# A two-layer streaming encoder step: mask rows sent between the latent queries, three norm biases added on VectorE, weight sums two products later

## The chip, the core and the metric

The kernel runs on one core of a Trainium2 chip. The metric is the device time of one launch in microseconds (us), the median of three runs, lower is better. TensorE (PE, with its weight loads as PEld), VectorE (DVE), ScalarE (ACT) and GpSimd (POOL) work through their own instruction streams in order; SyncE (SP) issues the DMAs in its own order.

## The reference, cut to what matters

1024 prompt frames and 64 sample frames (1088 rows, `T`) go through two layers with `D` = 1024. Layer 0 mixes by two head groups, of which A is latent attention with a rotary part and a chunk mask; layer 1 mixes by stick-breaking attention. After each mixer and each MLP stands a layer norm with a gain and a bias.

```python
# layer 0, group A: queries from a 768-wide latent, 8 heads of 64 + 32 rotary columns
q_a = (_rms_norm(h[..., :o1], g_q) @ w_uq).reshape(B, S, H_A, NOPE_DIM + ROPE_DIM)
q_a = jnp.concatenate([q_a[..., :NOPE_DIM], _rope(q_a[..., NOPE_DIM:], pos)], -1)
...
mask: (k_pos // CHUNK) <= (q_pos // CHUNK), CHUNK = 64
# every layer
x = LN(alpha * x + mixer(x) @ w_out)           # gain and bias of the mixer's norm
x = LN(alpha * x + square(relu(x @ w_up)) @ w_down)
...
LN(x) = (x - mean) * rsqrt(var + eps) * g + b
```

All products are in float32, made of three passes of a rounded high part and a low part (`H` and `L`): H*H, H*L and L*H.

## The kernel before, in words

A framework's scheduler orders the instructions of every engine by a timeline of its own, by the pools and slots of the tiles, and by hand-made "pace" marks (`after`) that hold an instruction behind a given matmul. Moving a line of the program therefore moves instructions on all engines near it.

`split` writes the high part on ScalarE (L152) and the low part on VectorE or, where told so, GpSimd (L153). `weight` loads a weight block by SP (L193) into the one buffer `wraw` and splits it.

**Latent queries.** `queries` makes, for the chunks of 384, 384 and 320 rows (`c`), the plain query columns (`nope`, four blocks `m`) and the rotary columns (`rotate`, three times, one a chunk). Each result is split into a tile `raw` of a ring of four buffers and written to DRAM: the plain parts to `qm_d` by one DMA (L481), the rotary ones to `qr_d` by two each (L506). The product takes the chunk mask from 32 more rows on each side of the rotary part: `qc` (from `qconst`) holds a 1 in the row of the query's chunk, the keys' rows a large negative number. These mask rows, too, are split into a `raw` tile and written to `qr_d`, four DMAs a chunk (L527), each for four heads. Before, they stand at the end of `queries`, behind the load of the first key weight `w_bk`. The products after that (keys of group B) copy their results by ScalarE into `kraw` (L621).

**Mixer output.** `out_proj` makes the 128-row blocks of the output product in the order `OUT_ORDER`, `[6, 4, 5, 0, 2, 1, 8, 3, 7]` in layer 0 and `[6, 4, 2, 0, 5, 1, 8, 3, 7]` in layer 1; block 8 holds the 64 sample rows, and the last two blocks are made together. `norm(t)` calls `layer_norm`: statistics on VectorE, the power for the deviation `rr` on GpSimd (L203), the mean taken off on ScalarE (L303), scaling by `rr` and the gain on VectorE (L304), the bias on GpSimd (L305), then a store and the transposes of `to_xq` on TensorE (L175, copied out at L239). Their result goes to the product up, which for the prompt rows uses a Strassen scheme: the sums and differences of its operand blocks are made on VectorE (L271, L276 to L279) and split.

**Product down.** `down` runs a Strassen scheme of seven products (`m` = 0 to 6) a group of 512 rows of the weight, for seven groups; `finish` does the eighth plainly. Product `q` = 7 `gr` + `m`. `strassen(q)` loads the next group's four weight blocks at `m` = 1 (`load_w`), makes the three sum blocks at `m` = 3 (`sum_w`: four subtractions, two on VectorE and two on GpSimd, L271, behind a mark of the product before), and prepares the operand splits one product ahead (`ahead`); results are added into accumulators by VectorE (L1493) or copied by ScalarE (L1495). The sums of the next group are first used by its product 2, whose splits are issued with product 1.

Tiles of the stages around `out_proj` and `down` are slots of a common store (`sl.take`, `sl.give`); their names in the trace (`sl`, `wo`, `xs`, `wL`, `wH`, `wraw`) are the slots', so a name says where a tile lies, not what it is.

Of the kernel before, what the change touches and what calls it, by code (L numbers as in the profile page):

```python
# [8 lines left out]
F32R = mybir.dt.float32r  # L9
AF = mybir.ActivationFunctionType  # L10
ALU = mybir.AluOpType
PSUM = bass.MemoryType.PSUM

P = 128
# [11 lines left out]
ROPE = 32  # L26
# [11 lines left out]
CHUNKS = [(0, 384), (384, 384), (768, 320)]  # L38
# [85 lines left out]
class Net:  # L124
# [153 lines left out]
        tt(s2, s1, a11, op=ALU.subtract)  # L278
        tt(a21, a12, s2, op=ALU.subtract)  # L279

    def layer_norm(self, pool, y, n, g, b, out, spread=True, square=None):


        nc = self.nc
        neg = self.tl(pool, [P, 1], "neg", 2)
        if square is not None:
            sm = self.tl(pool, [P, 2], "lnsum", 2)
            nc.scalar.activation(square[:n], y[:n], AF.Identity, accum_out=sm[:n, 0:1])
            nc.scalar.activation(neg[:n], sm[:n, 0:1], AF.Copy, scale=-1.0 / D)
            nc.scalar.activation(y[:n], y[:n], AF.Identity, bias=neg[:n])  # L290
            nc.scalar.activation(square[:n], y[:n], AF.Square, accum_out=sm[:n, 1:2])
            r = self.rstd(pool, sm[:n, 1:2], 1.0 / D, 1e-5, n)
        else:
            st = self.tl(pool, [P, 2, 6], "st", 2)
            for h in range(2):
                nc.vector.bn_stats(st[:n, h, :], y[:n, h * 512 : (h + 1) * 512])
            mv = self.tl(pool, [P, 2], "mv", 2)
            nc.vector.bn_aggr(mv[:n], st[:n])
            r = self.rstd(pool, mv[:n, 1:2], 1.0, 1e-5, n)
        if spread:  # L300
            if square is None:
                nc.vector.tensor_scalar(neg[:n], mv[:n, 0:1], -1.0, None, op0=ALU.mult)
                nc.scalar.activation(y[:n], y[:n], AF.Identity, bias=neg[:n])  # L303
            nc.vector.scalar_tensor_tensor(y[:n], y[:n], r[:n], g[:n], op0=ALU.mult, op1=ALU.mult)  # L304
            nc.gpsimd.tensor_tensor(y[:n], y[:n], b[:n], op=ALU.add)  # L305
            for o, r0 in out:
                nc.sync.dma_start(o, y[r0 : r0 + o.shape[0]])
        else:
            for c in (slice(0, 512), slice(512, D)):
                nc.vector.scalar_tensor_tensor(y[:n, c], y[:n, c], mv[:n, 0:1], g[:n, c], op0=ALU.subtract, op1=ALU.mult)  # L310
                nc.vector.scalar_tensor_tensor(y[:n, c], y[:n, c], r[:n], b[:n, c], op0=ALU.mult, op1=ALU.add)  # L311
                for o, r0 in out:
                    nc.sync.dma_start(o[:, c], y[r0 : r0 + o.shape[0], c])
# [148 lines left out]
    def queries(self, qn, uw):  # L462

        nc, io = self.nc, self.io
        up = self.pool("uq", "right")

        def load(m):
            if m < 4:
                raw = self.tl(up, [P, KQ, P], "uraw", 2)
                nc.sync.dma_start(raw, io["w_uq"][m])  # L470
                uw[m] = [self.tl(up, [P, KQ, P], f"u{m}{x}", 1, F32R) for x in "HL"]
                self.split(*uw[m], raw, mark=marks[-1])

        def uq(ps, m, c, n):
            marks.append(self.dense(ps[:, :n], uw[m], qn[c], KQ, 0, n))

        def nope(m, c):
            c0, n = CHUNKS[c]
            ps = self.ps("ds")
            uq(ps, m, c, n)  # L480
            nc.sync.dma_start(self.qm_d[m, :, :, c0 : c0 + n], self.parts(up, ps[:, :n], 4))  # L481

        def rotate(c):
            c0, n = CHUNKS[c]
            cs = self.tl(up, [P, 2, 384], "cs", 3)
            nc.sync.dma_start(cs[:, :, :n], io["rope_feat"][:, :, c0 : c0 + n])
            x12 = []
            for m in (4, 5):
                ps = self.ps("ds")
                uq(ps, m, c, n)  # L490
                x = self.tl(up, [P, 384], f"x{m}", 2)
                nc.scalar.activation(x[:, :n], ps[:, :n], AF.Copy)
                x12.append(x[:, :n])
            x1, x2 = x12
            cos, sin = cs[:, 0, :n], cs[:, 1, :n]
            m1, m2 = (self.tl(up, [P, 384], f"m{i}", 2)[:, :n] for i in range(2))
            nc.gpsimd.tensor_tensor(m1, x2, sin, op=ALU.mult)
            nc.gpsimd.tensor_tensor(m2, x1, sin, op=ALU.mult)
            nc.vector.tensor_tensor(x1, x1, cos, op=ALU.mult)
            nc.vector.tensor_tensor(x2, x2, cos, op=ALU.mult)  # L500
            nc.vector.tensor_tensor(x1, x1, m1, op=ALU.subtract)
            nc.vector.tensor_tensor(x2, x2, m2, op=ALU.add)
            for i, r in enumerate((x1, x2)):
                x = self.parts(up, r, 4)
                for o, base in ((0, 64), (1, 32)):
                    nc.sync.dma_start(self.qr_d[:, base + 16 * i : base + 16 * i + 16, :, c0 : c0 + n], x[o * 64 : o * 64 + 64])  # L506

        marks = []
        for m in range(4):
            if m < 3:  # L510
                rotate(m)
            if m == 0:
                load(0)
            for c in range(3):
                nope(m, c)
                if c == 1:
                    load(m + 1)
        late = marks[-3]
        first = self.weight(io["w_bk"][0], [P, KD, P], marks[-8], marks[-4])
        for c0, n in CHUNKS:  # L520
            qc = self.tl(up, [ROPE, 384], "qc", 2)
            self.after(nc.sync.dma_start(qc[:, :n], io["qconst"][:, c0 : c0 + n]), marks[-6])
            x = self.parts(up, qc[:, :n], 4)
            for i in range(2):
                src = x[:, i, :].unsqueeze(1).to_broadcast([ROPE, 4, n])
                for r in (96, 0):
                    nc.sync.dma_start(self.qr_d[:, r : r + 32, i, c0 : c0 + n].rearrange("e r t -> r e t"), src)  # L527
        up.release()
        return late, first

# [613 lines left out]
    def out_proj(self, layer, ws, ys, xres, xout, between):  # L1144
# [3 lines left out]
        nc, io, sl = self.nc, self.io, self.slots  # L1148
        order = OUT_ORDER[layer]
# [45 lines left out]

        def norm(t):
            t0, n = TOK[t]
            self.layer_norm(self.sm, ys[t], n, *gb, [(xout[t0 : t0 + n, :], 0)])
            self.to_xq(ys[t], t)
            sl.give(ys[t])  # L1200

# [4 lines left out]
        gb = []  # L1206
# [3 lines left out]
        for j, t in enumerate(order[:-2]):  # L1210
            load(order[j + 3] if j + 3 < len(order) else None)
            oH, oL, y = ops[t]
# [3 lines left out]
            for h in range(2):  # L1216
# [3 lines left out]
                else:  # L1220
                    for i in range(KD - 1 if early else 0, KD):
                        first = products(ps, t, i, h, early or i == 0, i == KD - 1)
                        if not gb:
                            gb = [self.bcast(sl, io[f"ln_mix_{x}"][layer : layer + 1, :], D, mark=first) for x in "gb"]
# [23 lines left out]
        for j, t in enumerate(two):  # L1248
            for h in range(2):
                add(t, h, banks[2 * j + h], False)  # L1250
            norm(t)
# [136 lines left out]
    def down(self, layer, xres, xout, last):  # L1388
# [4 lines left out]
        nc, io, sl = self.nc, self.io, self.slots  # L1393
# [9 lines left out]
        def load_w(gr, where=None):  # L1403
            B[gr] = [sl.take([2, 512], where=where) for _ in range(4)]
            for i in range(4):
                nc.sync.dma_start(B[gr][i], io["w_dn"][layer, gr, i // 2, i % 2])

        def sum_w(gr, where=None, mark=None):
            B[gr] += [sl.take([2, 512], where=where) for _ in range(3)]
            self.sums(*B[gr], nc.gpsimd, mark)  # L1410
# [30 lines left out]
        def place(gr):  # L1441


            return 1 if gr == NG - 2 else None
# [11 lines left out]
        def ahead_rest(gr):  # L1456
            A8[gr] = sl.take([12 * DEC], F32R), None
            A8[gr] = A8[gr][0], rest(gr, A8[gr][0])

        M1 = U2 = W1 = S0 = acc = None  # L1460
        marks = {}
# [35 lines left out]
        def strassen(q):  # L1497
            gr, m = divmod(q, 7)
            f0, end = gr == 0, gr == NG - 2
            if not end:  # L1500
                if m == 1:
                    load_w(gr + 1, place(gr + 1))
                elif m == 3:
                    sum_w(gr + 1, place(gr + 1), marks[q - 1])
                elif m == 4:
                    ahead_rest(gr + 1)
# [15 lines left out]
            for i in range(4):  # L1522
                ps = self.bank()
                c = slice(i * P, i * P + P)
                for k in range(2):
                    mark = self.mm3(ps, a[0][:, k, c], a[1][:, k, c], w[0][:, k, :], w[1][:, k, :], k == 0, k == 1)
# [34 lines left out]
        def finish():  # L1561
# [27 lines left out]
            for t in order:  # L1589
# [24 lines left out]
                else:  # L1614
# [4 lines left out]
                    self.turned.append(self.to_x(acc[t], rows[t]))  # L1619

        return prepare, strassen, finish, NQ

    def run(self):
# [204 lines left out]
```

## Time and profile before

| | before |
|---|---|
| median of 3 runs | 2842.57 us (2840.23 to 2843.23) |
| profiled execution | 2844.38 us, span 2842.6 us |
| TensorE busy | 2746.1 us, 97% |
| VectorE, ScalarE, GpSimd busy | 2169.5, 1515.0, 779.5 us |
| mean granted TensorE clock | 0.986 |

The span is the time from the first to the last instruction in the trace. A row of a timeline gives start, duration, engine, line, operation, the tile written and those read, and in brackets the engine's idle time before it with the instruction that ended the wait. The granted clock is 1.00 at full speed; where it drops, it is 0.50 for a while, and a mean over a stretch lies between.

### The profile page before, as it was taken

How to read it: one execution, taken by the hardware profiler on the slowest of the kernel's cores; microseconds unless marked ns; L12 is line 12 of the kernel's file. 1: busy time of each engine (PE TensorE's matmuls, PEld its weight loads, DVE VectorE, ACT ScalarE, POOL GpSimd, SP SyncE). 2: the span in 40 equal slices, each digit the busy share in tenths (PEclk: the TensorE clock that was granted, in tenths of full speed). 3: DMA queues.
4: the chain of work that ended last, by engine and by line, in shares of the span. 5: the costliest groups of instructions: out<-in, count | busy, mean ns of one | idle time of the engine just before them, and what ended most of it. 6: DMA issues, size and time to landing. Idle time of an engine off the chain costs nothing. (4 is left out here: it accounts for less than half of the span.)

```text
span 2842.6 us, 46984 instructions
## 1 busy us (share of the span) xinstructions
PE 2746.1 (97%) x16931; PEld 2507.9 (88%) x16931; DVE 2169.5 (76%) x3826; ACT 1515.0 (53%) x3106; POOL 779.5 (27%) x889
## 2 busy tenths in 40 slices
PE   9999999999999999999999999998999999999998
PEld 8999997878899998878789999998879999977876
DVE  4335677785867777999968887878677767689998
ACT  4226666883555555333257777778445555543331
POOL 3013333652200002322543343434241000122235
PEclk9999999999999999999999999999999999999999
DMA  6162234434234457344321111112242444654432
GB/s 196 40 176 70 62 95 97 100 104 146 86 131 137 138 170 261 117 151 134 107 93 59 51 55 51 51 54 98 67 152 86 152 148 131 234 167 144 158 115 84
DMA packets 228600, 331.47 MB, mean 117 GB/s; under 512 B 44720, under 2 KB 161104, under 8 KB 228368
## 3 DMA queue, kind: packets, MB, share of 16 engines
q1 hardware_dynamic: 228368, 328.48, 36.4%
q8 instruction: 134, 2.20, 0.3%
q14 instruction: 98, 0.80, 0.1%
HBM read 214.49 MB, written 109.99 MB: 114 GB/s over the span
## 5 line engine op out<-in xcount | busy, mean ns | idle before, releaser
L726 POOL TENSOR_TENSOR G<-G,S 128x384 f32<-128x384 f32 (+4 forms) x200 | 201.7, 1012 | 344.6 <-DVE S L723 119.5
L157 PE MATMUL d<-xH,wH 128*128 128x384 f32 (+1 forms) x784 | 263.6, 336 | 7.6 <-ACT kraw L621 5.2
L159 PE MATMUL d<-xH,wL 128*128 128x384 f32 (+1 forms) x784 | 262.2, 334 | 0.0
L158 PE MATMUL d<-xL,wH 128*128 128x384 f32 (+1 forms) x784 | 261.2, 333 | 0.0
L153 DVE TENSOR_TENSOR wtL<-t,wtH 128x512 fp32r<-128x512 f32 (+2 forms) x328 | 196.9, 618 | 46.4 <-ACT wtH L152 37.7
L152 ACT ACTIVATE wtH<-t 128x512 fp32r<-128x512 f32 (+2 forms) x328 | 170.4, 545 | 48.3 <-PE t L175 21.6
L790 PE MATMUL pv<-wtH,V 128*128 128x256 f32 (+1 forms) x624 | 159.2, 280 | 4.6 <-ACT o L750 3.2
L665 POOL TENSOR_TENSOR R<-R,inv 128x640 f32<-128x640 f32 (+6 forms) x100 | 115.4, 1166 | 171.3 <-DVE inv L664 100.3
L792 PE MATMUL pv<-wtL,V 128*128 128x256 f32 (+1 forms) x624 | 154.2, 288 | 8.1 <-DVE wtL L153 8.1
L157 PEld LDWEIGHTS d<-xH,wH 128*128 128x128 f32 x784 | 148.8, 190 | 11.9 <-ACT kraw L621 6.3
L723 DVE TENSOR_TENSOR_SCAN S<-S,own 128x513 f32<-128x513 f32 (+3 forms) x144 | 144.9, 1017 | 12.7 <-ACT S L716 9.7
L158 PEld LDWEIGHTS d<-xL,wH 128*128 128x128 f32 x784 | 148.7, 190 | 1.3
L159 PEld LDWEIGHTS d<-xH,wL 128*128 128x128 f32 x784 | 148.7, 190 | 1.2
L152 ACT ACTIVATE wo<-wo 128x1024 fp32r<-128x1024 f32 (+4 forms) x86 | 75.4, 884 | 111.7 <-DMA wo<-o 24.1
L792 PEld LDWEIGHTS pv<-wtL,V 128*128 128x128 f32 x624 | 120.2, 193 | 11.8 <-DVE wtL L153 10.3
L790 PEld LDWEIGHTS pv<-wtH,V 128*128 128x128 f32 x624 | 120.0, 192 | 9.7 <-ACT o L750 5.7
L175 PE MATMUL t<-ident,G 128*128 128x128 f32 x600 | 103.6, 278 | 14.5 <-POOL S L714 7.7
L658 PE MATMUL s<-kS,qH 128*128 128x384 f32 (+3 forms) x288 | 105.8, 369 | 2.7 <-DVE mx L681 1.6
L716 ACT ACTIVATE S<-s 128x384 f32<-128x384 f32 (+4 forms) x200 | 98.7, 494 | 15.1 <-PE s L658 12.4
L717 ACT ACTIVATE G<-s 128x384 f32<-128x384 f32 (+4 forms) x200 | 99.5, 497 | 0.1
L152 ACT ACTIVATE sl<-wo 128x1024 fp32r<-128x1024 f32 (+4 forms) x51 | 46.8, 922 | 94.5 <-DVE wo L271 22.3
L658 PE MATMUL s<-kS,qL 128*128 128x384 f32 (+3 forms) x288 | 96.8, 337 | 0.0
(1858 smaller groups left out, 9933.3 us busy)
## 6 DMA issues: line engine op xcount, KB each, us to landing
wo<-a_d SPq DMA_DIRECT2D x52, 512.0 KB, 4.3
a_d<-wo SPq DMA_DIRECT2D x32, 544.0 KB, 3.7
wo<-in_w_dn SPq DMA_DIRECT2D x32, 512.0 KB, 5.7
sl<-a_d SPq DMA_DIRECT2D x25, 512.0 KB, 3.6
wo<-in_w_up SPq DMA_DIRECT2D x21, 512.0 KB, 4.6
a_d<-sl SPq DMA_DIRECT2D x19, 544.0 KB, 3.9
sl<-in_w_up SPq DMA_DIRECT2D x17, 512.0 KB, 3.8
sl<-in_w_dn SPq DMA_DIRECT2D x17, 512.0 KB, 5.5
```

What stands on the lines that cost most here:

```text
L152: self.after(self.nc.scalar.activation(H, src, AF.Copy), mark)
L153: (engine or self.nc.vector).tensor_tensor(L, src, H.bitcast(F32), op=ALU.subtract)
L157: i = mm(out, aH, bH, start=first, stop=False)
L158: mm(out, aH, bL, start=False, stop=False)
L159: mm(out, aL, bH, start=False, stop=last)
L175: return self.nc.tensor.transpose(out, in_, self.ident[:n, :n])
L658: self.nc.tensor.matmul(ps[:, :n], q, k, start=i == 0, stop=i == len(passes) - 1)
L665: nc.gpsimd.tensor_tensor(R[:, :nk], R[:, :nk], inv.to_broadcast([P, nk]), op=ALU.mult)
L723: nc.vector.tensor_tensor_scan(s[r], s[r], own, carry, op0=ALU.mult, op1=ALU.max)
L726: nc.gpsimd.tensor_tensor(G[:, :n], G[:, :n], S[:, 1 : n + 1], op=ALU.mult)
L790: mm(out, v, wH[:, s : s + n], start=bi == 0 and s == 0, stop=False)
L792: mm(out, v, wL[:, s - n : s], start=False, stop=bi == len(banks) - 1 and j == bank[-1][0])
```

## The change

It has three parts. The mask rows become a function `mask_rows(c)`, called behind the middle chunk of the query blocks 1, 2 and 3, for chunks 0, 1 and 2, paced by the last product's mark; beside it, the first plain weight block is loaded from within the first `rotate`. The bias of the last three norms of the mixer (blocks 8, 3 and 7, in both layers) is added by VectorE. The sums of the next group's weights are made at product 5 of a group, where it was product 3.

```diff
-    def layer_norm(self, pool, y, n, g, b, out, spread=True, square=None):
+    def layer_norm(self, pool, y, n, g, b, out, spread=True, square=None, add=None):
...
-            nc.gpsimd.tensor_tensor(y[:n], y[:n], b[:n], op=ALU.add)
+            (add or nc.gpsimd).tensor_tensor(y[:n], y[:n], b[:n], op=ALU.add)
...
                 uq(ps, m, c, n)
+                if (m, c) == (4, 0):
+                    load(0)
...
+        def mask_rows(c):
+            c0, n = CHUNKS[c]
+            qc = self.tl(up, [ROPE, 384], "qc", 2)
+            nc.sync.dma_start(qc[:, :n], io["qconst"][:, c0 : c0 + n])
+            x = self.tl(up, [P, 2, 384], "raw", 4)[:ROPE, :, :n]
+            y = x.bitcast(F32R)
+            self.split(y[:, 0, :], y[:, 1, :], qc[:, :n], mark=marks[-1])
+            for i in range(2):
+                src = x[:, i, :].unsqueeze(1).to_broadcast([ROPE, 4, n])
+                for r in (96, 0):
+                    nc.sync.dma_start(self.qr_d[:, r : r + 32, i, c0 : c0 + n].rearrange("e r t -> r e t"), src)
...
             if m < 3:
                 rotate(m)
-            if m == 0:
-                load(0)
             for c in range(3):
                 nope(m, c)
                 if c == 1:
                     load(m + 1)
+                if c == 1 and m:
+                    mask_rows(m - 1)
         late = marks[-3]
         first = self.weight(io["w_bk"][0], [P, KD, P], marks[-8], marks[-4])
-        for c0, n in CHUNKS:
-            qc = self.tl(up, [ROPE, 384], "qc", 2)
-            self.after(nc.sync.dma_start(qc[:, :n], io["qconst"][:, c0 : c0 + n]), marks[-6])
-            x = self.parts(up, qc[:, :n], 4)
-            for i in range(2):
-                src = x[:, i, :].unsqueeze(1).to_broadcast([ROPE, 4, n])
-                for r in (96, 0):
-                    nc.sync.dma_start(self.qr_d[:, r : r + 32, i, c0 : c0 + n].rearrange("e r t -> r e t"), src)
...
-            self.layer_norm(self.sm, ys[t], n, *gb, [(xout[t0 : t0 + n, :], 0)])
+            self.layer_norm(self.sm, ys[t], n, *gb, [(xout[t0 : t0 + n, :], 0)], add=nc.vector if t in order[-3:] else None)
...
-                elif m == 3:
+                elif m == 5:
                     sum_w(gr + 1, place(gr + 1), marks[q - 1])
```

Where instructions move, three places show it. The first is ScalarE in the latent queries, from the last two chunks of block `m` = 1 to the second rotary pair; `raw<-x` is a rotary part, `raw<-s` and `raw<-d` are query parts, `raw<-qc` is a mask part, and `wH` is the split of `w_bk`. Before:

```order
L152 ACTIVATE raw_1677<-s_1658 128x384
L152 ACTIVATE raw_1706<-d_1687 128x320
L492 ACTIVATE x_302_1731<-s_1712 128x320
L152 ACTIVATE u3H_1820<-uraw_1818 128x768
L492 ACTIVATE x_304_1752<-d_1733 128x320
L152 ACTIVATE wH_325_1917<-wraw_1916 128x1024
L152 ACTIVATE raw_1762<-x_302_1731 128x320
```

And with the change:

```order
L152 ACTIVATE raw_1677<-s_1658 128x384
L152 ACTIVATE raw_1689<-qc_1687 32x384
L152 ACTIVATE raw_1715<-d_1696 128x320
L494 ACTIVATE x_304_1740<-s_1721 128x320
L152 ACTIVATE u3H_1829<-uraw_1827 128x768
L494 ACTIVATE x_306_1761<-d_1742 128x320
L152 ACTIVATE wH_331_1944<-wraw_1943 128x1024
```

A mask part has come in between the two query parts, and so takes the buffer of the ring that the second query part had. On SP's queue at the same place, before:

```order
L481 DMA qm_d<-raw_1677 256x1x384
L193 DMA wraw_1916<-in_w_bk 128x1024
L481 DMA qm_d<-raw_1706 256x1x320
L522 DMA qc_1922<-in_qconst 32x384
L522 DMA qc_1931<-in_qconst 32x384
L506 DMA qr_d<-raw_1762 4x32x320 x2
```

And with the change:

```order
L481 DMA qm_d<-raw_1677 256x1x384
L520 DMA qr_d<-raw_1689 32x4x384 x4
L481 DMA qm_d<-raw_1715 256x1x320
L513 DMA qc_1911<-in_qconst 32x320
L193 DMA wraw_1943<-in_w_bk 128x1024
L508 DMA qr_d<-raw_1771 4x32x320 x2
```

The load of `w_bk` has moved behind four mask writes, a query write and a load.

The second place is VectorE in the mixer's norm of the 64 sample rows in layer 1 (the tile `sl1_13`; `sl1_10` is the bias). Before:

```order
L304 SCALAR_TENSOR_TENSOR sl1_13_4983_24313<-sl1_13_4983_24313,rr_5025_24494,sl1_9_4953_24103 64x1024
L153 TENSOR_TENSOR wo1_6_5048_24649<-wo1_3_5046_24645,wo1_6_5048_24649 128x512
L153 TENSOR_TENSOR wo1_7_5049_24652<-wo1_3_5046_24645,wo1_7_5049_24652 128x512
L153 TENSOR_TENSOR wo1_10_5051_24658<-wo1_4_5047_24646,wo1_10_5051_24658 128x512
L153 TENSOR_TENSOR wo1_9_5050_24655<-wo1_4_5047_24646,wo1_9_5050_24655 128x512
```

And with the change:

```order
L304 SCALAR_TENSOR_TENSOR sl1_13_4983_24313<-sl1_13_4983_24313,rr_5025_24494,sl1_9_4953_24103 64x1024
L153 TENSOR_TENSOR wo1_6_5048_24649<-wo1_3_5046_24645,wo1_6_5048_24649 128x512
L153 TENSOR_TENSOR wo1_7_5049_24652<-wo1_3_5046_24645,wo1_7_5049_24652 128x512
L305 TENSOR_TENSOR sl1_13_4983_24313<-sl1_13_4983_24313,sl1_10_4954_24105 64x1024
L153 TENSOR_TENSOR wo1_10_5051_24658<-wo1_4_5047_24646,wo1_10_5051_24658 128x512
```

The bias stands on VectorE two splits behind the scaling; before it was in GpSimd's stream.

The third place is VectorE in the first group of the product down, layer 1: L1493 (L1499 with the change) adds a result to an accumulator, L271 is the first sum of the next group's weights, L153 a split. Before:

```order
L1493 SCALAR_TENSOR_TENSOR sl_2_5575_28955<-sl_2_5575_28955,d_29055 128x512
L271 TENSOR_TENSOR wo_5_5614_29126<-wo_1_5594_29031,sl_4_5593_29030 128x1024
L153 TENSOR_TENSOR sl_6_5620_29139<-sl_10_5543_28760,wo_17_5619_29138 128x1024
L1493 SCALAR_TENSOR_TENSOR sl_17_5576_28956<-sl_17_5576_28956,t_29063 128x512
L1493 SCALAR_TENSOR_TENSOR wo_12_5577_28957<-wo_12_5577_28957,s_29071 128x512
```

And with the change:

```order
L1499 SCALAR_TENSOR_TENSOR sl_2_5575_28955<-sl_2_5575_28955,d_29055 128x512
L1499 SCALAR_TENSOR_TENSOR sl_17_5576_28956<-sl_17_5576_28956,t_29063 128x512
L153 TENSOR_TENSOR wo_7_5626_29180<-sl_21_5550_28800,sl_11_5625_29179 128x1024
L1499 SCALAR_TENSOR_TENSOR wo_12_5577_28957<-wo_12_5577_28957,s_29071 128x512
L1499 SCALAR_TENSOR_TENSOR sl_3_5582_28962<-sl_3_5582_28962,t_29079 128x512
```

The sum has left this place, and the split of `sl_10_5543` stands earlier, ahead of these rows.

## The prediction

> **What bounds the kernel now.** I read the totals first, then the granted clock by stage, then TensorE's idle gaps in order of time, and last the engines that TensorE waits for.
>
> ```profile
> span 2842.6 us, 46984 instructions
> PE 2746.1 (97%) x16931; PEld 2507.9 (88%) x16931; DVE 2169.5 (76%) x3826; ACT 1515.0 (53%) x3106; POOL 779.5 (27%) x889
> ```
>
> TensorE is busy in 97% of the span, so whatever an edit does to another engine is worth only what it takes out of the remaining 96 us of TensorE idle time (2842.6 - 2746.1), or out of time at a lowered clock. The next view is the table of stretches; its columns are the stretch, its length, busy us of PE, PEld, DVE, ACT, POOL, then granted clock, DMA share and GB/s.
>
> ```profile
> 203.50:212.00 8.50, 5.91 (x25) 5.64 (x25) 4.96 (x10) 5.71 (x13) 2.78 (x3) 0.60 0.93 253
> 212.00:228.00 16.00, 13.13 (x69) 12.82 (x70) 4.67 (x10) 7.56 (x18) 4.86 (x9) 0.89 0.29 101
> 758.00:771.00 13.00, 9.21 (x53) 8.59 (x52) 8.73 (x8) 8.91 (x14) 5.82 (x2) 0.74 0.21 82
> 2107.00:2125.00 18.00, 13.39 (x57) 10.54 (x56) 10.98 (x12) 9.02 (x15) 8.75 (x2) 0.81 0.14 42
> 2140.00:2154.00 14.00, 11.53 (x69) 10.75 (x68) 12.85 (x12) 9.97 (x14) 5.53 (x3) 0.76 0.19 76
> 2486.00:2506.00 20.00, 16.20 (x64) 12.55 (x63) 17.98 (x14) 11.57 (x16) 9.03 (x3) 0.91 0.91 294
> 1107.00:1122.00 15.00, 13.43 (x59) 10.22 (x58) 12.56 (x12) 10.45 (x14) 6.49 (x3) 1.00 1.00 319
> 2506.00:2785.00 279.00, 279.00 (x1204) 223.00 (x1204) 264.38 (x297) 99.06 (x105) 76.97 (x37) 1.00 0.40 133
> ```
>
> Six of these stretches hold a piece at half clock. Its length is the length of the stretch times (1 - clock) / 0.5: 6.8, 3.5, 6.8, 6.8, 6.7 and 3.6 us. By the matmuls' starts, 1.8 times as far apart there, the pieces begin at 203.7, 224.2, 763.5, 2115.2, 2145.9 and 2500.9. Half of what TensorE is busy in a piece is lost. The last row is the other extreme: in the steady part of the product down, layer 1, TensorE never idles, and no edit can gain there. TensorE's timeline names the gaps in those stretches (start, duration, then in brackets the idle time before it and who ended it).
>
> ```profile
> 181.17 0.44 PE L157 MATMUL s<-xH,wH 128*128 128x384 f32 x1 [0.17 <-DVE raw L153]
> 205.88 0.64 PE L157 MATMUL d<-xH,wH 128*128 128x320 f32 x1 [4.25 <-ACT kraw L621]
> 223.45 0.55 PE L175 MATMUL t<-ident,kraw 128*128 128x128 f32 x3 [2.87 <-ACT kraw L621]
> 763.00 1.50 PE L175 MATMUL t<-ident,xs 128*128 128x128 f32 x8 [2.78 <-POOL xs L305]
> 765.51 1.97 PE L175 MATMUL t<-ident,xs 128*128 128x128 f32 x8 [1.01 <-POOL xs L305]
> 1120.17 0.50 PE L1518 MATMUL pv<-wo,wH 128*128 128x512 f32 x1 [1.57 <-DVE wo L1493]
> 2117.20 1.11 PE L175 MATMUL t<-ident,sl 64*128 64x64 f32 x8 [4.61 <-POOL sl L305]
> 2145.46 0.39 PE L157 MATMUL s<-wo,sl 128*128 128x272 f32 x1 [1.84 <-ACT wo L152]
> 2146.98 1.97 PE L175 MATMUL t<-ident,sl 128*128 128x128 f32 x8 [0.63 <-POOL sl L305]
> 2501.31 0.79 PE L157 MATMUL pv<-wo,wH 128*128 128x512 f32 x1 [3.80 <-ACT sl L1495]
> ```
>
> They sum to 23.4 us without the first row. Each part of the change aims at some of them.
>
> **Part 1: mask rows.** Before, the three mask parts follow the last latent query, with four writes each on SP's queue. Rows picked from the timelines of SP's queue and of ScalarE:
>
> ```profile
> 153.58 4.25 SPq L506 DMA_DIRECT2D qr_d<-raw  x4
> 159.78 2.43 SPq L193 DMA_DIRECT2D wraw<-in_w_bk  x1
> 198.63 0.97 SPq L522 DMA_DIRECT2D qc<-in_qconst  x1
> 201.88 0.47 ACT L152 ACTIVATE raw<-qc 32x320 fp32r<-32x320 f32 x1 [10.11 <-DMA qc<-in_qconst]
> 162.28 0.44 ACT L152 ACTIVATE raw<-d 128x320 fp32r<-128x320 f32 x1 [6.38 <-DMA qr_d<-raw]
> 169.67 1.06 ACT L152 ACTIVATE wH<-wraw 128x1024 fp32r<-128x1024 f32 x1 [5.56 <-DMA wraw<-in_w_bk]
> 180.15 0.44 ACT L152 ACTIVATE raw<-s 128x320 fp32r<-128x320 f32 x1 [7.95 <-DMA qr_d<-raw]
> 183.43 0.49 ACT L152 ACTIVATE raw<-d 128x384 fp32r<-128x384 f32 x1 [2.84 <-DMA qr_d<-raw]
> ```
>
> The third load of `qc` is issued only at 198.63, behind earlier mask writes; ScalarE waits 10.11 us for it, and the key splits and the `kraw` copies (L621) queue behind. That is the cause of the gaps of 4.25 and 2.87 us. The first piece holds 4.6 us of work (203.7 + 6.8 - 205.88) and loses 2.3; the second is all work and loses 1.7. All of it gone would be 4.25 + 2.87 + 2.3 + 1.7 = 11.1 us.
>
> The price is in the last four rows. The mask part uses the ring of four `raw` buffers, in which latent queries and rotary parts already wait for writes to land. At 181.17 TensorE was already just touched (0.17 us): no slack is left there.
>
> The mask part takes the buffer that the query part used to take (free at 162.28), and the query part needs the next one, whose rotary write lands some 3.3 us later, as the second pair's two landings show (183.43 - 180.15). On SP the load of `w_bk` now stands behind four mask writes and a query write (the order is shown with the change); it was issued at 159.78 and landed at 169.67. I replay it: the first query part waits to 166, a stall of 0.9; `w_bk` lands about 174 and delays the second rotary pair by some 4 us, so that its landings move from 180.15 and 183.43 to about 184 and 188. The query part that waited for the first now waits for the second, since the mask part takes the first one's buffer. TensorE's product of 181.17, held by that query part, would start at about 188.4: 7.2 us of stalls in sum (0.9 of them at 166), and half clock behind the last for one short piece (half of 3.5 and its edge) 2 more: +9.2. Part 1 in sum is 9.2 - 11.1 = -1.9 us. Its ends are -11.1 (the replayed stalls are hidden) and +5 (a fourth such wait, with the 7.95 of the row at 180.15 in full).
>
> **Part 2: bias of the last three norms.** The first two rows are layer 0's, the others layer 1's.
>
> ```profile
> 758.27 2.48 DVE L304 SCALAR_TENSOR_TENSOR xs<-xs,rr,wH 128x1024 f32<-128x1024 f32 x2 [0.83 <-ACT xs L303]
> 759.63 5.82 POOL L305 TENSOR_TENSOR xs<-xs,xs 128x1024 f32<-128x1024 f32 x2 [3.53 <-DVE xs L304]
> 2107.05 1.28 DVE L304 SCALAR_TENSOR_TENSOR sl<-sl,rr,sl 64x1024 f32<-64x1024 f32 x1 [0.44 <-POOL rr L203]
> 2108.26 2.48 DVE L153 TENSOR_TENSOR wo<-wo,wo 128x512 fp32r<-128x512 f32 x4
> 2108.41 8.73 POOL L305 TENSOR_TENSOR sl<-sl,sl 64x1024 f32<-64x1024 f32 x1 [1.39 <-DVE sl L304]
> 2113.67 1.27 DVE L153 TENSOR_TENSOR wo<-sl,wo 128x1088 fp32r<-128x1088 f32 x1
> 2139.08 3.38 POOL L305 TENSOR_TENSOR sl<-sl,sl 128x1024 f32<-128x1024 f32 x1 [2.14 <-DVE sl L304]
> ```
>
> An add of two operands in VectorE takes 1.27 us for 1088 columns, so I take 1.2 for 1024. Layer 0: the two norms' scalings end at 760.75, the adds at 762.0 and 763.2, instead of 765.45. TensorE, idle from 760.22, starts its transposes at 762.0 and is through the second set at about 764.6, against 767.1: -2.5. The half-clock piece that follows holds 6.8 - 1.0 = 5.8 us of work and loses 2.9; the remaining gap of 1.8 us is as long as the one of 1.84 that has half clock behind it at 2145, and hardly longer than that of 1.57 at 1120, whose stretch shows clock 1.00. Between the two I take half of it: -1.4. Together -3.9, with ends -2.5 and -5.4. The Trainium skill, "TensorE: Matmul & The Clock Gate" (What's actually happening), has the clock halved after an idle window of about 3.4 us. Gaps of 1.84 and 2.87 us sufficed here, so the trace disagrees; by the rule this term would be -5.4, and the sum 1.5 us lower.
>
> Layer 1, the row of 64 tokens (t = 8): the add stands two short splits behind the scaling, 2108.3 + 2 x 0.62 + 1.2 = 2110.7; TensorE stops only at 2112.6 (2117.20 - 4.61). The gap of 4.61 goes, and with it the half-clock piece, with 4.8 us of work (2115.2 + 6.8 - 2117.2): -4.6 - 2.4 = -7.0. The splits behind the add come 1.2 us later; they are covered, since TensorE's next wait is the transpose itself. GpSimd's 8.73 us were no work: the add began at 2108.41, VectorE's run of two-operand adds ended at 2114.94 (2113.67 + 1.27), and GpSimd ended 2.2 us after that, at 2117.14. The Trainium skill's "SBUF — State Buffer" (who interferes with whom) has an exclusive lock here: GpSimd's read is blocked while VectorE reads two operands. The trace agrees, and the rule also speaks against this part: two more adds on VectorE can block the power for `rr` (GpSimd, L203) of the next norm, by 1.2 us on the path; the sum by it would be 1.2 us higher.
>
> The last two norms of layer 1: the first add ended at 2142.46 and ends on VectorE at about 2141.9; the second ends at about 2145.7, against 2146.93. That is -1.2 for the second set of transposes, less a little because four products that stood before them now follow. I take -1.0; half clock stays, since a gap of 2.1 us stays. Ends: -4.5 (half clock goes too) and +2 (VectorE, busy for 12.85 of 14 us there, delivers a split late). Part 2: -3.9 - 7.0 - 1.0 = -11.9.
>
> **Part 3: sums of the next weights.** The first group of layer 1:
>
> ```profile
> 2488.92 1.22 DVE L271 TENSOR_TENSOR wo<-wo,sl 128x1024 f32<-128x1024 f32 x1
> 2489.09 3.32 POOL L271 TENSOR_TENSOR wraw<-sl,wo 128x1024 f32<-128x1024 f32 x1 [3.97 <-DMA sl<-in_w_dn]
> 2490.06 3.43 DVE L153 TENSOR_TENSOR sl<-sl,wo 128x1024 fp32r<-128x1024 f32 x1
> 2493.52 1.06 ACT L152 ACTIVATE sl<-sl 128x1024 fp32r<-128x1024 f32 x1 [4.21 <-DVE sl L153]
> 1111.01 2.83 DVE L271 TENSOR_TENSOR xs<-wo,wraw 128x1024 f32<-128x1024 f32 x1
> ```
>
> The sum (1.22) and the split that GpSimd's sum slows (3.43 instead of about 1.2) stand ahead of the buffer that ScalarE waits 4.21 us for; from there its chain runs to the copy that ends TensorE's gap at 2501.31.
>
> After the change the sum is gone from there, and the split stands earlier. VectorE is 1.22 + 3.43 - 1.2 = 3.4 us ahead, so 3.4 of the 3.80 go, and the half-clock piece, 3.2 us of work behind 2501.31, gives 1.6: -5.0. In layer 0 the sum at 1111.01 is followed by slack, and of the 1.57 I count 0.6. In the steady groups the sums still run, beside a TensorE that is never idle; at 5.6 us a product (24 matmuls of 279 / 1204 = 0.23 each) they have three products, 17 us, for two sums on each engine, about 1.2 x 2 + 3.3 x 2 = 9. They are priced at nothing; were that cover gone, the rival below applies. The three buffers of the sums are taken later, so all later buffers change places: 0, with ends of 2 either way. Part 3: -5.0 - 0.6 = -5.6.
>
> **Sum.** -1.9 - 11.9 - 5.6 = -19.4 us. The profiled execution took 2844.4, its span and 1.8 around it; this is 1.8 above the median, 2842.6. From the median: 2823.
>
> **Rivals.**
> - *The mask rows cost nothing.* The ring's waits stay on ScalarE, whose idle time before the rows above (6.38, 5.56, 7.95) is large. Against it: the 0.17 at 181.17. Without the 9.2: 2814.
> - *VectorE becomes late* in the last norms: its 12.85 of 14 us speak for it; that GpSimd's slowing of its other adds goes speaks against. Then the gaps at 763 and 2147 stay as they are, -4.9 is not realised, and some 3 us more come from splits (two adds of 1.2 ahead of them): 2831.
> - *The weights' sums come late in the steady part.* A wait for the last sum at each of the 10 later group changes, 2 us each, is +20: 2843, no change. It needs the 8 us of slack gone.
> - *The time is given back.* The gaps go, but TensorE meets the next wait sooner, as where a DMA sets the pace (share 0.91 in the stretch of 2486 and 1.00 in that of 1107): half the gain, 2833.
> - *Slower: the ring.* If each mask part holds its buffer until its own writes land behind a rotary pair, three turns of the ring wait 8.7 us each on TensorE (162.28 - 153.58, the first pair from issue to landing), +26, plus half of a 6.8 piece after each, +10: +36, where I have 9.2. Part 1 is then +25, and the whole 2850. The point from which it decides is two and a half such waits; there the whole is even. Against it: the third mask part takes a mask part's buffer, not a rotary one's.
>
> **How the numbers follow.** Forecast 0.50, free mask rows 0.16, VectorE late 0.10, given back 0.08, sums late 0.08, slower by the ring 0.08. About 0.2% (5.7 us) is what a measurement can tell from no change. The first four end below 2837: 0.84, of which I move 0.03 to no change, since given back may be more than half. The range runs from 2812, the free mask rows with 2 us from the other ends, to 2840, which leaves out the slower case and most of the late sums; the forecast's own range is 2816 to 2831.
>
> **What would show it.** In the profile after, no idle time at the `kraw` copies, but waits of TensorE on `raw` around 160 to 190; no GpSimd L305 in the three norms, transposes of the 64 tokens without a wait and clock 1.00 behind them; no gap and no half clock in the first group of layer 1. The prediction is wrong if TensorE waits for `raw` by over 20 us in sum, or for a split in the group changes of the product down.

## The result and the profile after

The changed kernel takes 2822.61 us (median, 2818.91 to 2824.68), against 2841.4 for the kernel before in the same comparison: a ratio of 0.9933 (0.9916 to 0.9950), 19 us faster, where 2823 was forecast. The profiled execution took 2818.91, 3.7 below its median, while that of before, 2844.38, lies 3.0 above the median of this comparison; so the two traces differ by 25.5 us, 6.7 more than the medians.

```profile
span 2817.1 us, 46994 instructions
PE 2731.1 (97%) x16931; PEld 2495.5 (89%) x16931; DVE 2159.4 (77%) x3832; ACT 1515.0 (54%) x3106; POOL 760.2 (27%) x883
```

TensorE's idle time fell from 96 to 86 us, and its busy time by 15: the same matmuls, fewer of them at half clock. The table of stretches of the kernel after (columns as before):

```profile
160.00:190.00 30.00, 21.52 (x126) 20.62 (x125) 8.80 (x15) 6.33 (x13) 7.34 (x10) 0.95 0.58 154
190.00:212.00 22.00, 22.00 (x122) 22.00 (x122) 7.40 (x13) 7.00 (x14) 5.55 (x3) 0.91 0.79 231
755.00:768.00 13.00, 11.12 (x90) 10.72 (x89) 10.85 (x11) 10.88 (x17) 0.00 (x0) 1.00 0.21 82
2095.00:2112.00 17.00, 16.89 (x91) 13.79 (x89) 16.56 (x20) 10.08 (x17) 1.31 (x2) 1.00 0.31 93
2118.00:2135.00 17.00, 15.32 (x123) 14.92 (x122) 16.24 (x19) 12.58 (x21) 3.70 (x2) 1.00 0.16 63
2462.00:2485.00 23.00, 23.00 (x101) 18.39 (x100) 16.80 (x18) 18.73 (x29) 6.02 (x4) 1.00 0.96 314
2755.00:2775.00 20.00, 17.98 (x70) 13.45 (x69) 19.30 (x29) 1.15 (x1) 10.28 (x8) 0.91 0.16 53
```

Rows 3 to 6 answer to the stages of the norms and of the first group in layer 1: full clock in all four. The first two rows hold the latent queries, where half clock has moved forward. The last row is the end of the product down in layer 1, where a new half-clock piece stands. TensorE's gaps in these stretches after:

```profile
166.52 0.44 PE L157 MATMUL d<-qn384H,u2H 128*128 128x384 f32 x1 [1.23 <-DVE raw L153]
177.81 0.45 PE L157 MATMUL s<-qn384H,u3H 128*128 128x384 f32 x1 [2.14 <-DVE raw L153]
188.96 0.69 PE L157 MATMUL s<-xH,wH 128*128 128x384 f32 x1 [5.11 <-DVE raw L153]
759.58 2.20 PE L175 MATMUL t<-ident,xs 128*128 128x128 f32 x16 [1.81 <-DVE xs L305]
2125.30 1.06 PE L175 MATMUL t<-ident,sl 128*128 128x128 f32 x8 [0.29 <-DVE sl L305]
2127.76 1.06 PE L175 MATMUL t<-ident,sl 128*128 128x128 f32 x8 [1.39 <-DVE sl L305]
2763.88 0.64 PE L157 MATMUL s<-wo,sl 128*128 128x512 f32 x1 [2.02 <-DVE wo L1497]
```

The gaps at the key copies, the 4.61 of the sample rows and the 3.80 of the first group in layer 1 have gone. I lined up the two traces by the n-th matmul of each, and took how far the start lies ahead of that of before (negative is earlier), at the ends of the stages:

| stage, by the times of before | forecast | change and before | one part alone |
|---|---|---|---|
| start-up, to 130 | 0 | -1.1 | |
| latent queries and key copies, 130 to 260 | -1.9 | +0.7 | mask rows: +1.3 |
| last norms, layer 0, 757 to 770 | -3.9 | -4.5 | bias: -4.5 |
| first group, layer 0, 1090 to 1125 | -0.6 | -0.9 | sums: -1.1 |
| norm of the sample rows, layer 1, 2112 to 2125 | -7.0 | -6.8 | bias: -6.8 |
| last two norms, layer 1, 2125 to 2160 | -1.0 | -3.9 | bias: -3.8 |
| first group, layer 1, 2480 to 2510 | -5.0 | -5.5 | sums: -5.5 |
| end of the product down, layer 1, 2780 to 2800 | 0 | +2.7 | sums: +2.7 |

These stages make -19.3 of the 25.5 us between the two traces. Most of the rest lies in stages that no part edits: -2.0 from 260 to 757 and -1.6 from 1480 to 2112, where half-clock pieces of before are missing (the clock from 425 to 440 was 0.89 before and 1.00 after, from 450 to 465 it was 0.77 and 0.89). The kernels with one part alone gained 0.3 to 2.2 us from 260 to 757 too, so one trace tells a stage to about 2 us.

### The profile page after: what moved, and what is told of

It is laid out like the page before. It is cut to its first block, busy times and chain, and to the rows that moved or that the text cites. A ratio compares the mean times of both kernels' runs of the same rounds, so it can differ in the third digit from the quotient of the medians.

```text
span 2817.1 us, 46994 instructions
## 1 busy us (share of the span) xinstructions
PE 2731.1 (97%) x16931; PEld 2495.5 (89%) x16931; DVE 2159.4 (77%) x3832; ACT 1515.0 (54%) x3106; POOL 760.2 (27%) x883
## 5 line engine op out<-in xcount | busy, mean ns | idle before, releaser
L153 DVE TENSOR_TENSOR wtL<-t,wtH 128x512 fp32r<-128x512 f32 (+2 forms) x328 | 197.0, 618 | 45.0 <-ACT wtH L152 36.2
L152 ACT ACTIVATE wo<-wo 128x1024 fp32r<-128x1024 f32 (+4 forms) x91 | 81.8, 907 | 125.7 <-PE d L158 28.2
L175 PE MATMUL t<-ident,G 128*128 128x128 f32 x600 | 103.4, 277 | 14.8 <-POOL S L720 7.2
L203 POOL TENSOR_TENSOR rr<-rv,mhalf 128x1 f32<-128x1 f32 (+1 forms) x54 | 37.8, 703 | 215.9 <-DVE neg L302 140.6
```

The costliest lines, as they stand in the source:

```text
L152: self.after(self.nc.scalar.activation(H, src, AF.Copy), mark)
L153: (engine or self.nc.vector).tensor_tensor(L, src, H.bitcast(F32), op=ALU.subtract)
L175: return self.nc.tensor.transpose(out, in_, self.ident[:n, :n])
```

## The experiments

**Each part alone.** Three kernels with one part of the change each. Their edits are the hunks of the diff above; `sums_only`, for one, is

```diff
-                elif m == 3:
+                elif m == 5:
                     sum_w(gr + 1, place(gr + 1), marks[q - 1])
```

> Only the first part of the change: the mask rows come in between the latent queries. Theory A (the parts add up, and this one pays for what it saves): the gaps of 4.25 and 2.87 us at the key copies go, but TensorE waits about 1.2, 2.1 and 5.1 us for split query parts between 160 and 190 us, with half clock behind the last; the time stays within 3 us of before. Rival (the mask rows carry a good share of the 19 us): 8 to 11 us faster than before.

> Only the second part: the bias of the last three norms on VectorE. Theory A: 15 us faster than before (4.6 at the norms of layer 0, 6.8 at the 64 rows of layer 1, 3.9 at its last two blocks), no half clock behind these norms. Rival (VectorE gets late, and part of it comes from the other parts' new order): 8 us or less.

> Only the third part: the sums of the next weights at product 5. Theory A: the gap of 3.8 us in the first group of layer 1 goes with its half clock (5.5 us), layer 0 gives 1 to 2, and 2 to 3 us are given back at the end of the product down of layer 1, where VectorE's additions come late: 4 to 5 us faster than before. Rival (sums late in the steady groups): no faster than before, with waits of TensorE for a split at the changes of groups.

Measured against 2841.6: the mask rows alone 2839.5 (ratio 0.9992, 0.9983 to 1.0001), no difference that can be told; the bias alone 2829.6 (0.9948, 0.9935 to 0.9962); the sums alone 2835.6 (0.9979, 0.9970 to 0.9988). By medians that is -2.1, -12.0 and -6.0, in sum -20.1, beside -18.8 for the whole. By the ratios it is 0.08 + 0.52 + 0.21 = 0.81%, beside 0.67% (0.50 to 0.84): the parts add up within the intervals. Theory A holds for the three; by medians the bias gave some 3 us less than expected (by the ratio 14.8, as expected), the sums 1 to 2 more. The last column of the table is from these traces. The mask rows alone show the wait that the change shows:

```profile
189.88 0.69 PE L157 MATMUL s<-xH,wH 128*128 128x384 f32 x1 [5.09 <-DVE raw L153]
```

**Where the mask rows stand.** The same first part, with the call one chunk later:

```diff
-                if c == 1 and m:
+                if c == 2 and m:
                     mask_rows(m - 1)
```

> Only the first part, and the mask rows called after the third chunk of each block instead of the second, so that on ScalarE and in the ring of four buffers each stands behind the query parts, and the load of the first key weight stands ahead of its writes on SP's queue. Theory A (the waits of the change come from the place in the ring and on the queue): the waits of 2.1 and 5.1 us go, at most one of 1 us stays, and the kernel is 8 to 11 us faster than before. Rival (twelve more writes among the queries cost by themselves, through the DMA engines): TensorE waits as in the run with the mask part alone, and the time is that of before.

Measured 2835.1, ratio 0.9977 (0.9967 to 0.9988): 6.5 faster than before, and not the 2 of the other place, but short of the 8 to 11 expected; its interval still touches that of the other place. In its trace the stage from 130 to 260 is 8.4 us shorter than before. ScalarE's timeline, first of the change and then of this kernel, at the same work:

```profile
161.08 0.52 ACT L152 ACTIVATE raw<-qc 32x384 fp32r<-32x384 f32 x1 [6.26 <-DMA qr_d<-raw]
165.50 0.44 ACT L152 ACTIVATE raw<-d 128x320 fp32r<-128x320 f32 x1 [3.90 <-DMA qr_d<-raw]
174.17 1.06 ACT L152 ACTIVATE wH<-wraw 128x1024 fp32r<-128x1024 f32 x1 [6.84 <-DMA wraw<-in_w_bk]
184.63 0.52 ACT L152 ACTIVATE raw<-qc 32x384 fp32r<-32x384 f32 x1 [7.93 <-DMA qr_d<-raw]
187.95 0.44 ACT L152 ACTIVATE raw<-s 128x320 fp32r<-128x320 f32 x1 [2.80 <-DMA qr_d<-raw]
```

```profile
159.80 0.44 ACT L152 ACTIVATE raw<-d 128x320 fp32r<-128x320 f32 x1 [6.11 <-DMA qr_d<-raw]
163.89 0.53 ACT L152 ACTIVATE raw<-qc 32x384 fp32r<-32x384 f32 x1 [3.65 <-DMA qr_d<-raw]
167.38 1.06 ACT L152 ACTIVATE wH<-wraw 128x1024 fp32r<-128x1024 f32 x1 [1.59 <-DMA wraw<-in_w_bk]
178.28 0.44 ACT L152 ACTIVATE raw<-s 128x320 fp32r<-128x320 f32 x1 [6.80 <-DMA qr_d<-raw]
```

The query part (`raw<-d`, then `raw<-s`) takes the first buffer that comes free, at 159.80 and 178.28, and the mask part the next; `w_bk` is split at 167.38 instead of 174.17. TensorE waits for a query part only once, for 0.51 us. The same twelve writes stand among the queries here, and the waits are gone: the rival falls. This run moves the place in the ring and that on SP's queue together; how the cost of 8.5 us (1.23 + 2.14 + 5.11) divides between them wasn't tried.

**The whole change with the later mask rows, and with mask rows that need no ring.** The first kernel joins that edit with the other two parts. The second writes the rows from their own tile, and sends them one query block earlier:

```diff
-            nc.sync.dma_start(qc[:, :n], io["qconst"][:, c0 : c0 + n])
-            x = self.tl(up, [P, 2, 384], "raw", 4)[:ROPE, :, :n]
-            y = x.bitcast(F32R)
-            self.split(y[:, 0, :], y[:, 1, :], qc[:, :n], mark=marks[-1])
-            for i in range(2):
-                src = x[:, i, :].unsqueeze(1).to_broadcast([ROPE, 4, n])
+            self.after(nc.sync.dma_start(qc[:, :n], io["qconst"][:, c0 : c0 + n]), marks[-1])
+            for i, x in enumerate((qc, zero)):
+                src = x[:, :n].unsqueeze(1).to_broadcast([ROPE, 4, n])
...
+        zero = self.tl(up, [ROPE, 384], "zero", 1)
+        nc.gpsimd.memset(zero, 0.0)
...
-                if c == 1 and m:
-                    mask_rows(m - 1)
+                if c == 2 and m < 3:
+                    mask_rows(m)
```

> The whole change, with the mask rows called after the third chunk of each block. Theory A (the parts add up): -6.5 for the mask rows in this place, -12.0 for the norms, -6.0 for the sums, as they measured alone: 2817 us, 4 to 5 below the change. Rival (what is saved early is given back at later waits): no faster than the change, 2822.

> The whole change, but the mask rows, which are ones and zeros, are written from the loaded tile itself and from a tile of zeros: no split, no buffer of the ring, nothing on ScalarE and VectorE. Theory A (the ring is what the mask rows cost): no wait of TensorE for a split query part between 150 and 200 us, the key copies 5 us earlier than in the run with the mask rows late, 9 to 11 us for this part, 2812 to 2816 us. Rival (the copies of the first keys wait for something else, such as the load of the cached keys at the end of SP's queue): the same as with the mask rows late, 2817.

Measured against 2841.2: 2812.4 (0.9897, 0.9884 to 0.9911) and 2811.6 (0.9893, 0.9880 to 0.9907). Both beat the change, by 10 and 11 us, and cannot be told from each other; the first is some 5 us below the 2817 expected. Nothing was given back at later waits: by the ratios the parts alone make 0.23 + 0.52 + 0.21 = 0.96%, the first kernel 1.03% (0.89 to 1.16). In the stage from 130 to 260 the second kernel gained 8.3 us in its trace and the first 6.6, and there the next limit stands:

```profile
196.25 0.86 ACT L152 ACTIVATE kS<-kraw 64x256 fp32r<-64x256 f32 x2 [6.74 <-DMA kraw<-in_cache_bkT]
206.90 0.45 PE L157 MATMUL s<-xH,wH 128*128 128x384 f32 x1 [0.62 <-ACT kraw L626]
```

Both rows are the second kernel's. ScalarE now waits for the cached keys, whose load stands behind the query writes on SP's queue; TensorE's gap at the key copies is down to 0.62 (2.56 with the mask rows late). The other half of theory A fails: with no mask part in the ring TensorE still waits for query parts, 0.32 us at 162.98 and

```profile
174.08 0.44 PE L157 MATMUL s<-qn384H,u3H 128*128 128x384 f32 x1 [1.95 <-DVE raw L153]
181.90 0.44 PE L157 MATMUL s<-xH,wH 128*128 128x384 f32 x1 [1.79 <-DVE raw L153]
```

where the first kernel waits 0.65. TensorE came to this stage 2.2 us sooner than before, but ScalarE waits for the rotary writes as it did then (7.92 us for `qr_d` at 180.88), and the product that started at 181.17 before starts at 181.90. So the mask parts are not all that the ring waits for, and the time is the one that the rival named, the same as with the mask rows late.

**When the sums are made.** Product 6 alone, and product 4 in the second kernel above:

> Only the third part, one product later still, at product 6. Theory A (in the steady groups the sums are hidden, and the gain is in the first group alone): as with product 5, 5 to 7 us faster than before, since two products of 5.6 us still cover a chain of about 9. Rival (the sums are already near to being late): waits of TensorE for a split at the changes of groups, 1 to 3 us each, so that the gain is gone or turned round.

> The run with the mask rows written straight from their tile, and the sums of the next weights at product 4 instead of 5. Theory A (any place outside the first products of the first group gives the gain; the 2 to 3 us lost at the end of the product down of layer 1 come from the order of the last group, not from the sums): within 3 us of 2811.6. Rival (two products later is too late for the last group): 2 to 4 us faster, with no gap of 2 us near 2765. Another rival (product 4 still runs into the first group's additions): part of the gap of 3.8 us of the first group is back, 3 to 5 us slower.

Product 6 measured 2836.1 (0.9980, 0.9971 to 0.9989), the same as product 5; its trace has no wait of TensorE within the steady groups. So the cover that I priced the sums by is there even with one product less. Product 4 measured 2821.7 (0.9934, 0.9922 to 0.9947), 10 us slower than the same kernel with product 5, and so against theory A; the third expectation had 3 to 5. Two gaps come up in the first groups of both layers, each with half clock behind:

```profile
1105.13 0.50 PE L157 MATMUL t<-wo,wo 128*128 128x512 f32 x1 [3.36 <-ACT wo L152]
2476.90 0.50 PE L157 MATMUL d<-wo,wo 128*128 128x512 f32 x1 [3.35 <-ACT wo L152]
```

The cause that the third expectation named is not seen: VectorE's first subtraction stands behind each of the two gaps (at 1106.25 and 2478.02; with product 5 the former is at 1105.06), and what TensorE waits for is a split on ScalarE. The edit to product 4 also puts the sums ahead of `ahead_rest`, another preparation for the next group, while with 5 and 6 they stand behind it. So the gain of this part is not in lateness as such; whether the sums' product, their order against `ahead_rest` or the slots decide it was not tried. The 2 to 3 us lost near the end of layer 1 appear with the sums at 4, 5 and 6 alike (the trace lost 2.0 to 2.9 us there), and 0 to 1.2 in the kernels with the sums at 3. That they come with this part is shown; why the order of the last group changes is open.

**Which norms count.** Only the sample rows' bias, then all nine norms:

```diff
-add=nc.vector if t in order[-3:] else None
+add=nc.vector if t in order[-3:-2] else None
```

```diff
-add=nc.vector if t in order[-3:] else None
+add=nc.vector
```

> Only the second part, and of it only the bias of the 64 sample rows, in both layers. Theory A: the wait of 4.61 us and the half clock behind it in layer 1 are all of it, 6.8 us faster than before; the norms of the last two blocks keep their waits of 2.78 and 1.01 us in layer 0 and 0.63 in layer 1. Rival (the three adds on GpSimd hold each other up, so that taking one away helps the next): 9 us or more.

> Only the second part, with the bias of all nine norms of the mixer on VectorE. Theory A (only the norms whose transposes TensorE waits for count, the others are hidden): as with the last three, 12 us faster than before, within 3 us. Rival (VectorE is the next bound of this stage, and six more adds of 1.2 us put it late): a gain of 6 us or less, with new waits of TensorE around 700 or 2090 us.

The sample rows alone measured 2835.6 (0.9975, 0.9966 to 0.9984), 5.6 us by medians; in its trace the stage of the sample rows gave 6.8, and the norms after them kept gaps of 2.78, 1.03 and 0.75. Theory A holds. All nine measured 2830.2 (0.9961, 0.9948 to 0.9975) beside 0.9948 (0.9935 to 0.9962) for the last three: the intervals overlap, and by its time theory A holds. Among these stages the trace shows a difference in one place, the last two norms of layer 1, where the gain of 3.8 us is lost: VectorE makes both scalings and then both adds there, so that both sets of transposes wait for the first add behind two scalings.

```profile
2133.55 3.65 PE L175 MATMUL t<-ident,sl 128*128 128x128 f32 x16 [3.61 <-DVE sl L305]
```

## Why the prediction was right, step by step

**The sum** was -19.4 and measured -18.8 by medians; the parts, -1.9, -11.9 and -5.6, measured -2.1, -12.0 and -6.0 alone. They agree more closely than the terms below, which is in part luck: 2.9 us more than forecast at the last norms of layer 1 and 2.7 given back at its end cancel.

**Part 1.** The replay of the ring held nearly to the row: I had the first query part at 166, `w_bk` landing at 174, the second pair's landings at 184 and 188 and TensorE's product at 188.4. The trace has 165.50, 174.17, 184.63, 187.95 and 188.96, and stalls of 8.5 us where I had 7.2. So the first part was worth nothing that can be told by itself, and the profile of before told so: the three rows in which ScalarE waited for `qr_d` said that every buffer of the ring was in use. In the stage the traces show +0.7 instead of -1.9: the stalls were 1.3 longer, and the half-clock piece behind the last one, which ends at 193.8 (clock 0.51 from 187 to 194), holds 4.9 us of work and loses 2.4, where I had counted 2. The rest is no more than the stage varies: it was 1.8 and 0.5 us longer than before in the kernels with the bias alone and the sums alone, whose mask rows stand as before. The rival that the mask rows cost nothing was the behaviour of another place of the same call, 2812 with the other parts.

**Part 2.** The adds on VectorE took what I had taken, and both places of the largest terms came out: in layer 0 -4.5 for -3.9, for the half clock of which I had kept half went entirely, while the gaps shrank by 2.0 (from 2.78 and 1.01 to 1.81) and not by 2.5; at the sample rows -6.8 for -7.0.

```profile
758.22 2.35 DVE L305 TENSOR_TENSOR xs<-xs,xs 128x1024 f32<-128x1024 f32 x2
2098.75 1.21 DVE L305 TENSOR_TENSOR sl<-sl,sl 64x1024 f32<-64x1024 f32 x1
2123.94 1.22 DVE L305 TENSOR_TENSOR sl<-sl,sl 128x1024 f32<-128x1024 f32 x1
2126.39 1.22 DVE L305 TENSOR_TENSOR sl<-sl,sl 128x1024 f32<-128x1024 f32 x1
```

The step that failed is the last two norms of layer 1, "half clock stays, since a gap of 2.1 us stays": the gap was 0.29 and 1.39, the stretch has clock 1.00, and -3.9 came for -1.0. I had put no term for GpSimd's first add holding up VectorE in its turn. A sum between the two scalings took 2.52 us beside that add (before, first row), and 0.43 with the change:

```profile
2140.24 2.52 DVE L277 TENSOR_TENSOR wo<-wo 128x272 f32<-128x272 f32 x1
2123.59 0.43 DVE L277 TENSOR_TENSOR wo<-wo 128x272 f32<-128x272 f32 x1
```

The last scaling so begins 4.01 us behind the one before it, where it was 5.48. The price that I gave in a sentence from the Trainium skill ("SBUF — State Buffer", Who interferes with whom), that the adds on VectorE might block the power for `rr`, was not paid there: the power of the last norm took 0.67 us, and 0.75 before. That of the norm ahead of it took 4.60 (3.33 before), but the nearest bias add had ended 16 us earlier, and VectorE waited 0.45 us for it.

**Part 3.** -5.5 in the first group of layer 1 for -5.0, by the mechanism foretold (no gap, clock 1.00 in the row of 2462). The slots' change of places, "0, with ends of 2", was not 0 if it is what stands behind this: about +2.7 at the end of layer 1, where a gap of 0.99 us grew to 2.02 and got half clock behind it, and -1.2 from 1125 to 1480 in the change's trace, which the run with the sums alone (+0.1 there) does not show.

The rivals with VectorE late or with the sums late did not occur: the norms' gaps shrank as shown, and TensorE was busy for 270.00 of 270.00 us in the steady part of layer 1 (2485 to 2755). The slower rival, the ring, was real in kind, but two of the three waits were short.

## What to carry to other kernels

Work that is off the critical path but shares a ring of buffers with work on it is not free: put it behind the critical user of each buffer, not ahead, and look at the queue of its writes too; here one chunk later was worth 4 us with the mask rows alone and 10 in the whole change, by medians. When one engine's small operation sits between two stages of the bounding engine, price it by the trace's longest case (8.73 us), not by its usual one (2.40), and count the half-clock piece that the gap brings. Moving a filler operation by one step may cost more than it gained (10 us from product 5 to 4, where 6 were gained from 3 to 5): read the order around the first use, and measure both neighbours.

## What the runs showed of the hardware that was not expected

Whether a gap of about 2 us brings on half clock is not settled by its length. Before the first latent query, TensorE waits 1.94 us for the first weight in two kernels; the stretch around it, in the change and then in the kernel with the mask rows from their own tile:

```profile
131.02 0.44 PE L157 MATMUL s<-qn0H,u0H 128*128 128x384 f32 x1 [1.94 <-ACT u0H L152]
129.00:138.00 9.00, 7.06 (x33) 6.99 (x32) 6.15 (x10) 3.64 (x8) 1.98 (x2) 0.81 0.37 113
```

```profile
129.95 0.44 PE L157 MATMUL s<-qn0H,u0H 128*128 128x384 f32 x1 [1.94 <-ACT u0H L152]
129.00:138.00 9.00, 8.05 (x47) 8.05 (x48) 6.08 (x9) 3.06 (x6) 1.97 (x2) 1.00 0.67 207
```

The clock is 0.81 in the one (a half-clock piece of 3.4 us) and 1.00 in the other. In the change a gap of 2.61 us at 1092.51 passed at clock 1.00 (from 1085 to 1100), and one of 2.02 at 2763.88 did not (0.91 in the row above). The Trainium skill, "TensorE: Matmul & The Clock Gate" (What's actually happening), has a window of about 3.4 us that runs free of the work: the pieces' length agrees, and so does the same gap with two outcomes; an idle time of a whole window was not needed in any of these.

The records of the granted clock in the traces tell what differs. In each trace they change only at steps of 3.413 us, counted from the first change. The gap of 1.94 us stands in all twelve traces. In nine, of which the change is one (129.07 to 131.02, in the step from 129.00 to 132.41), at least 1.84 us of it lie within one step, and half clock follows. In three, of which the other kernel is one (128.01 to 129.95, cut by a step's end at 129.42), at most 1.80 do, and none follows. The 2.61 us are cut too, at 1091.56, and the 2.02 are not. Over all twelve traces, from 30 to 2795 us, TensorE was busy for under 45% of 83 steps at full clock, and half clock followed each of them; it followed 38 of 229 steps with 45 to 70%, and 3 of 8977 with more. So what counts here is how much idle time falls into one step, more than how long the gap is; the 38 say that busy time alone does not settle it near the border.
